# Attention heads on half the array: two heads, or two score maps, issued by turns on the two halves

## The chip, the cores and the metric

The kernel runs on one core of a Trainium2 chip. Times are device microseconds (us) of that core for one execution of the whole program; the time of a kernel is the median of its runs. The profile is a recording of one further execution. In it the engines are called PE (TensorE, matmuls), PEld (the weight loads of TensorE), DVE (VectorE), ACT (ScalarE), POOL (GpSimd) and SP (SyncE, which here issues the DMA transfers); "SPq" is SP's queue. L715 is line 715 of the kernel.

## The reference, cut to what matters

Two unrelated models run one after the other on 256 tokens of width 1024: `first_block` (called block 1 below) and `second_block` (block 2). Block 1 has two layers; in each, three kinds of attention work on one projection of the input, and their outputs, side by side, go through `w_o`. Only this part of block 1 is touched:

```python
def first_block(x, ...):
    h = x
    for i in range(DEPTH):                       # DEPTH = 2
        u = h @ w_in[i]
        u_mla, u_diff, u_sb = jnp.split(u, [MLA_IN, MLA_IN + DIFF_IN], axis=-1)
        y_mla = mla_mixer(u_mla, ...)            # 4 heads, 64 values a head
        y_diff = diff_mixer(u_diff, ...)         # 4 heads, two maps of 64 rows each, 128 values a head
        y_sb = sb_mixer(u_sb)                    # 4 heads of 64
        mix = jnp.concatenate([y_mla, y_diff, y_sb], axis=-1) @ w_o[i]
        h = layer_norm(DEEPNORM_ALPHA * h + mix, ln1_g[i], ln1_b[i])
        ffn = grouped_moe(h, ...)                # 16 experts
        ...

# diff_mixer, one head:
        a = attn_map(q1, k[0]) - lam * attn_map(q2, k[1])   # two softmax maps
        return jnp.einsum('bhqk,bhkd->bhqd', a, v)          # then an rms norm over 128 values

# sb_mixer (stick-breaking), one head:
        z = jnp.einsum('bhqd,bhkd->bhqk', qb, k) * scale
        log_fail = jnp.where(strict, jax.nn.log_sigmoid(-z), 0.0)
        later = lax.cumsum(log_fail, axis=3, reverse=True) - log_fail
        w = jnp.where(strict, jnp.exp(jax.nn.log_sigmoid(z) + later), 0.0)
        return jnp.einsum('bhqk,bhkd->bhqd', w, v)
```

The mask lets a query of the first 128 tokens see only the first 128 keys, so a score map is 128 queries x 256 keys for the later half and 128 x 128 for the earlier: 384 columns on 128 partitions.

## The kernel before

`mixers(l)` in block 1 makes the attention of layer l. Scores and values are fp32 matmuls (two records each in the trace, merged as x2); projections are products of operands split into a high and a low part, three matmuls each (`mm3`, lines 272 to 274).

**The heads as units.** Each head is a generator: `mla` and `sb` heads in turn first, then the four `diff` heads. A unit yields after each of its steps. A multi-latent head (`mla`) has three steps: scores and softmax; three transposes (`turn`, line 297) and a copy to SBUF (line 650); values. A stick-breaking head (`sb`) has scores with a mask product added (lines 715 to 718) and a log-sigmoid on ACT and DVE; the sums over later keys (lines 728 to 730) and an exponential; values (lines 736 and 737). A difference head (`diff`) has its first map's scores and softmax, its second map's, the combination on DVE, the transposes, the values and the sum of squares by ACT, and the product that sums over the partitions (line 704) with the norm. `scores` is on lines 631 and 632, `values` on 654 and 655, the bias add of a difference map on 686, `softmax` on 636 to 642.

**Halves of the array.** A stick-breaking head has 64 channels, so its scores contract over 64 rows, `qk[r]` with r the upper or the lower 64 partitions; the two maps of a difference head lie on the two halves in the same way. The values of a multi-latent or a stick-breaking head are 64 columns wide, and their output goes to the upper or lower 64 partitions `o[r]` of its own PSUM bank.

**What is drawn between the steps.** `flow(units, DM)` keeps DM = 3 units alive and takes a step of each in turn. After each step, `filling()` gives FM[l] steps on average (0.7 in layer 0, 0.6 in layer 1): first `diff_v` and `diff_in` (the projections that the difference heads need), then `project`, the product with w_o, one row block of the heads at a time in the order WO_ORDER as soon as `heads` has them. `diff(h)` draws on `filling()` until its own projection is there. In layer 0 the steps also draw 0.5 of a step of `t5`, which builds the position bias.

**Order, PSUM, weights.** The order of the code is what a scheduler starts from; it decides each engine's own order. `aux()` gives one of four PSUM banks to every score, transpose, sum or value tile; projections have the four others. Weights arrive by DMA in slots of SBUF, issued by SP in order, and are split into high and low by ACT (line 236) and DVE or POOL (line 267) some way ahead. `drop("mla")`, in the last stick-breaking head's last step, frees the four slots that the attention holds, and weight loads go there next. After `filling()` has run out come the layer norm, the expert stage and, after two layers, block 2.

## Time and profile before

| | |
|---|---|
| median of 3 runs | 1607.31 us (1604.68 to 1607.84) |
| the profiled execution | 1608.48 us, of which the span of the trace is 1606.7 us |
| PE busy | 1535.0 us, 96% of the span, 10998 matmul records |
| DVE busy | 824.1 us, 51% |
| ACT busy | 645.3 us, 40% |
| POOL busy | 201.0 us, 13% |
| DMA | 216 GB/s read and written over the span |

The attention heads of block 1 run from 54 to 152 us in the first layer and from 486 to 575 us in the second. A span is counted from the first to the last record of the trace; the execution's own time has 1.8 us more. Busy shares are means over stages that have different limits, and a matmul's end is modelled, so that the duration of a matmul record overlaps the next one's; the distance from one start to the next is what a matmul holds the engine for.

### The profile page before, as it was taken

Reading aid. Unit: us, or ns where it says so; the run is one execution under the profiler, and the core shown is the slowest. Engines: PE = TensorE matmul, PEld = TensorE weight load, DVE = VectorE, ACT = ScalarE, POOL = GpSimd, SP = SyncE. Lnnn points to the kernel's source line nnn. Section 1 sums busy time; section 2 is a strip of 40 time slices with the busy share of each in tenths; the row PEclk is TensorE's granted clock in tenths of the full one; section 3 lists DMA queues with packets and bytes.
Section 4 is the critical chain, followed back from the end, with each engine's and each line's share of the span. In section 5 each row is a group of like instructions: output and inputs, shape, how many; then the busy total and the mean of one; then the engine's idle time right before and its main releaser. Section 6 shows DMA issues by size and latency. Waiting matters only on the chain.

```text
span 1606.7 us, 26861 instructions
## 1 busy us (share of the span) xinstructions
PE 1535.0 (96%) x10998; PEld 1170.3 (73%) x10998; DVE 824.1 (51%) x1624; ACT 645.3 (40%) x1309; POOL 201.0 (13%) x236
## 2 busy tenths in 40 slices
PE   7999999989799999998997899899999999999999
PEld 7788744444287876454436787588999998799998
DVE  6677612212345772131216776536666666576665
ACT  5466411111136642110115674545444455554443
POOL 0130100000101001000003631301111023220000
PEclk9999999999999999999999999689999999999999
DMA  8335899999462489999943111025555452254540
GB/s 348 140 131 186 338 407 421 380 421 421 145 239 71 159 315 356 422 382 419 421 206 140 66 54 56 1 83 191 173 184 184 157 192 79 79 180 164 184 156 27
DMA packets 50034, 348.77 MB, mean 217 GB/s; under 512 B 5616, under 2 KB 6896, under 8 KB 8688
## 3 DMA queue, kind: packets, MB, share of 16 engines
q1 hardware_dynamic: 49904, 346.97, 56.2%
q8 instruction: 90, 1.47, 0.4%
q14 instruction: 40, 0.33, 0.1%
HBM read 345.90 MB, written 1.05 MB: 216 GB/s over the span
## 4 chain that ended last, share of the span: by engine, by line
PE 45%; DVE 4%; ACT 2%; POOL 1%; issue 1%; DVEq 0%; POOLq 0%; ACTq 0%
PE bank L274 10%; PE bank L272 10%; PE bank L273 10%; PE bank L1033 3%; PE bank L1067 2%; DVE ring L267 1%; PE aux L1507 1%; PE aux L297 1%; PE bank L994 1%; PE aux L1491 1%; PE aux L2008 1%; PE bank L1639 1%; ACT ring L236 1%; PE bank L1769 1%; PE aux L1986 1%
## 5 line engine op out<-in xcount | busy, mean ns | idle before, releaser
L236 ACT ACTIVATE ring<-ring 128x1024 fp32r<-128x1024 f32 (+3 forms) x188 | 185.8, 994 | 188.6 <-PE bank L274 166.6
L267 DVE TENSOR_TENSOR ring<-ring,ring 128x1024 fp32r<-128x1024 f32 x145 | 180.4, 1244 | 93.5 <-ACT ring L236 93.1
L272 PE MATMUL bank<-uh,ring 128*128 128x272 f32 (+1 forms) x744 | 218.6, 294 | 2.3 <-ACT ring L236 2.3
L274 PE MATMUL bank<-uh,ring 128*128 128x272 f32 (+1 forms) x744 | 215.5, 290 | 4.2 <-DVE ring L267 3.7
L273 PE MATMUL bank<-ul,ring 128*128 128x272 f32 (+1 forms) x744 | 215.0, 289 | 0.0
L274 PEld LDWEIGHTS bank<-uh,ring 128*128 128x128 f32 x744 | 141.4, 190 | 6.0 <-DVE ring L267 5.6
L272 PEld LDWEIGHTS bank<-uh,ring 128*128 128x128 f32 x744 | 141.3, 190 | 5.1 <-ACT ring L236 2.5
L273 PEld LDWEIGHTS bank<-ul,ring 128*128 128x128 f32 x744 | 141.2, 190 | 0.9 <-issue 0.2
L274 PE MATMUL bank<-rh,ring 128*128 128x272 f32 (+1 forms) x496 | 141.6, 286 | 0.0
L272 PE MATMUL bank<-rh,ring 128*128 128x272 f32 (+1 forms) x496 | 141.4, 285 | 0.0
L273 PE MATMUL bank<-rl,ring 128*128 128x272 f32 (+1 forms) x496 | 140.9, 284 | 0.0
L1039 DVE TENSOR_TENSOR hid<-hid,bank 128x512 f32<-128x512 f32 x16 | 11.0, 687 | 186.4 <-PE bank L1033 173.7
L273 PEld LDWEIGHTS bank<-rl,ring 128*128 128x128 f32 x496 | 93.8, 189 | 0.0
L272 PEld LDWEIGHTS bank<-rh,ring 128*128 128x128 f32 x496 | 93.2, 188 | 0.0
L274 PEld LDWEIGHTS bank<-rh,ring 128*128 128x128 f32 x496 | 93.0, 187 | 0.0
L267 POOL TENSOR_TENSOR ring<-ring,ring 128x1024 fp32r<-128x1024 f32 x6 | 14.5, 2436 | 574.4 <-ACT ring L236 574.4
L1257 POOL TENSOR_TENSOR fr<-fr 128x272 f32<-128x272 f32 (+1 forms) x64 | 40.2, 629 | 287.3 <-DVE fr L245 283.4
L245 DVE SCALAR_TENSOR_TENSOR big<-bank,gs,big 128x512 fp32r<-128x512 f32 x32 | 24.0, 750 | 99.2 <-ACT big L236 97.5
L267 DVE TENSOR_TENSOR ring<-wsp,ring 128x1024 fp32r<-128x1024 f32 x41 | 52.8, 1287 | 26.1 <-ACT ring L236 26.1
L236 ACT ACTIVATE ring<-wsp 128x1024 fp32r<-128x1024 f32 x41 | 43.4, 1058 | 55.4 <-PE bank L274 54.2
L236 ACT ACTIVATE big<-bank,gs 128x512 fp32r<-128x512 f32 x32 | 22.0, 688 | 108.0 <-PE bank L1067 107.7
L994 PE MATMUL bank<-P,hnat 128*128 128x128 f32 x512 | 63.6, 286 | 0.0
(677 smaller groups left out, 3431.4 us busy)
## 6 DMA issues: line engine op xcount, KB each, us to landing
ring<-w_ff SPq DMA_DIRECT2D x50, 1024.0 KB, 4.9
ring<-w_down SPq DMA_DIRECT2D x34, 1024.0 KB, 12.9
ring<-w_up SPq DMA_DIRECT2D x30, 1024.0 KB, 13.0
ring<-w_gate SPq DMA_DIRECT2D x29, 1024.0 KB, 10.4
big<-w_gate SPq DMA_DIRECT2D x24, 1024.0 KB, 16.4
big<-w_up SPq DMA_DIRECT2D x18, 1024.0 KB, 10.9
big<-w_down SPq DMA_DIRECT2D x17, 1024.0 KB, 11.8
wsp<-w_ff SPq DMA_DIRECT2D x14, 1024.0 KB, 4.8
```

The source lines that it names most:

```text
L236: return self.nc.scalar.activation(out, in_, func, **kw)
L245: return (eng or self.nc.vector).scalar_tensor_tensor(out, in0, s, in1, op0=op0, op1=op1, **kw)
L267: (eng or self.nc.vector).tensor_sub(l, src, h.bitcast(F32))
L272: mm(out, lhs[0], rhs[0], start=first, stop=False)
L273: mm(out, lhs[0], rhs[1], start=False, stop=False)
L274: mm(out, lhs[1], rhs[0], start=False, stop=last)
L297: self.nc.tensor.transpose(out, in_, self.ident[:k, :k])
L994: mm(b[:, j * M2:(j + 1) * M2], h[:, t, (k + j) * 128:(k + j + 1) * 128], P[:, t], start=t == 0, stop=t == 1)
L1033: mm(b[e * 64:e * 64 + CAP], xg[:, k, e * CAP:(e + 1) * CAP], w[:, (2 * k + e) * 512:(2 * k + e + 1) * 512], start=k == 0, stop=k == 7)
L1067: mm(yb[n][e * 64:e * 64 + CAP], hT[:, k, e * 64:e * 64 + CAP], w[:, o:o + 512], start=k == 0, stop=k == 3)
L1257: nc.gpsimd.tensor_mul(r, r, r)
L1491: nc.tensor.matmul(b[:, :N2], qw[r, j, self.hcols(t)], qw[r, 4], start=True, stop=True)
```

## The change

The heads of a kind go in pairs as one unit: `mla(hp)` and `sb(hp)` take heads 2hp and 2hp + 1, and a step of a difference head now issues the scores of both maps. `scores` and `values` take lists: first the 256-column matmuls of both halves, then the 128-column ones of both, so that neighbours in the code lie on different halves of the array. The values of a pair go to the two halves of one PSUM bank, and are split into high and low by one copy and one subtraction over 128 partitions, where two heads had one each over 64. The multi-latent units keep the scores of a pair in two steps, and the transposes in two; a stick-breaking pair keeps its two sum steps. The exponentials of the four multi-latent heads each have a place of their own (`me`, four in place of two). There are 38 unit steps in place of 48 in a layer, and FM goes from 0.7 and 0.6 to 0.88 and 0.75.

```diff
--- before.py
+++ after.py
@@ -58,7 +58,7 @@
 PJ = 3
 PL = 2
 PN = 2
-FM = (0.7, 0.6)
+FM = (0.88, 0.75)
 WPA = ((1, 3, 5, 7, 9, 11), ())
 WO_ORDER = [0, 1, 6, 7, 2, 3, 4, 5]
 T5_THR = [-90, -63, -45, -31, -22, -15, -11, -7, -6, -5, -4, -3, -2, -1, 0,
@@ -487,7 +487,7 @@
             vv = p1.tile([128, 2, 512], F32, name="vv")
             slot = self.slot(hold="mla")
             cn = slot[:, 0:768].rearrange("p (a s) -> p a s", a=3)
-            me = [slot[:, 768 + i * 384:768 + (i + 1) * 384] for i in range(2)]
+            me = [slot[:, i * 384:(i + 1) * 384] for i in range(4)]
             slot = self.slot(hold="mla").rearrange("p (a h s) -> p a h s", a=2, h=4)
             kt, qt = slot[:, 0], slot[:, 1]
             slot = self.slot(hold="mla")
@@ -627,10 +627,13 @@
                                     self.drop("hT")
                             yield
 
-            def scores(q, k, s):
-                mm(s[:, 0:256], q[:, 128:256], k, start=True, stop=True)
-                mm(s[:, 256:384], q[:, 0:128], k[:, 0:128], start=True, stop=True)
-                return s[:, 0:384]
+            def scores(qs, ks, ss):
+
+                for q, k, s in zip(qs, ks, ss):
+                    mm(s[:, 0:256], q[:, 128:256], k, start=True, stop=True)
+                for q, k, s in zip(qs, ks, ss):
+                    mm(s[:, 256:384], q[:, 0:128], k[:, 0:128], start=True, stop=True)
+                return [s[:, 0:384] for s in ss]
 
             def softmax(s, e):
 
@@ -650,26 +653,31 @@
                 nc.scalar.copy(PT, tp[:, :384])
                 return PT
 
-            def values(out, v, cols, PT):
-                mm(out[:, 0:256], v[:, 0, cols], PT[:, 0:256], start=True, stop=False)
-                mm(out[:, 128:256], v[:, 1, cols], PT[:, 256:384], start=False, stop=True)
-
-            def mla(h_):
-                s = scores(qt[:, h_], kt[:, h_], self.aux())
-                nc.vector.memset(self.masked(s), NEG)
-                e = me[h_ % 2]
-                rs = softmax(s, e)
-                self.ts(e[:, 0:256], e[:, 0:256], rs[:, 0:1])
-                self.ts(e[:, 256:384], e[:, 256:384], rs[:, 1:2])
-                yield
-                PT = turn(e)
-                yield
+            def values(outs, v, cols, PTs):
+                for out, cc, PT in zip(outs, cols, PTs):
+                    mm(out[:, 0:256], v[:, 0, cc], PT[:, 0:256], start=True, stop=False)
+                for out, cc, PT in zip(outs, cols, PTs):
+                    mm(out[:, 128:256], v[:, 1, cc], PT[:, 256:384], start=False, stop=True)
+
+            halves = [slice(64 * j, 64 * j + 64) for j in range(2)]
+
+            def mla(hp):
+                PTs = []
+                for h_ in (2 * hp, 2 * hp + 1):
+                    s, = scores([qt[:, h_]], [kt[:, h_]], [self.aux()])
+                    nc.vector.memset(self.masked(s), NEG)
+                    e = me[h_]
+                    rs = softmax(s, e)
+                    self.ts(e[:, 0:256], e[:, 0:256], rs[:, 0:1])
+                    self.ts(e[:, 256:384], e[:, 256:384], rs[:, 1:2])
+                    yield
+                for h_ in (2 * hp, 2 * hp + 1):
+                    PTs.append(turn(me[h_]))
+                    yield
                 o = self.aux()
-                r = slice(64 * (h_ % 2), 64 * (h_ % 2) + 64)
-                values(o[r], vm, slice(64 * h_, 64 * h_ + 64), PT)
-                self.split(yh[r, h_ // 2], yl[r, h_ // 2], o[r, 0:256])
-                if h_ % 2:
-                    heads.append(h_ // 2)
+                values([o[r] for r in halves], vm, [slice(64 * h_, 64 * h_ + 64) for h_ in (2 * hp, 2 * hp + 1)], PTs)
+                self.split(yh[:, hp], yl[:, hp], o[:, 0:256])
+                heads.append(hp)
                 yield
 
             def diff(h_):
@@ -679,13 +687,11 @@
                     next(t5)
                 q, k = dqk[h_][:, 0], dqk[h_][:, 1]
                 es = []
-                for i in range(2):
-                    r = slice(64 * i, 64 * i + 64)
-                    s = scores(q[r], k[r], self.aux())
+                for s in scores([q[r] for r in halves], [k[r] for r in halves], [self.aux(), self.aux()]):
                     e = p2.tile([128, 384], F32, name="de", bufs=4)
                     nc.vector.tensor_add(e, s, self.bias[:, h_])
                     es.append((e, softmax(e, e)))
-                    yield
+                yield
                 (e1, r1), (e2, r2) = es
                 lr = p2.tile([128, 2], F32, name="lr", bufs=3)
                 self.ts(lr, r2, lam)
@@ -696,7 +702,7 @@
                 PT = turn(e1)
                 yield
                 o = self.aux()
-                values(o, vv, slice(128 * h_, 128 * h_ + 128), PT)
+                values([o], vv, [slice(128 * h_, 128 * h_ + 128)], [PT])
                 sq = p2.tile([128, S], F32, name="osq", bufs=2)
                 self.act(sq, o[:, 0:256], AF.Square)
                 yield
@@ -708,37 +714,33 @@
                 heads.append(2 + h_)
                 yield
 
-            def sb(h_):
-                hp, j = h_ // 2, h_ % 2
-                r = slice(64 * j, 64 * j + 64)
-                z = self.aux()[:, 0:384]
-                mm(z[:, 0:256], qk[r, 1, hp, 0:128], qk[r, 0, hp], start=True, stop=False)
-                mm(z[:, 0:128], self.ident, self.c["future"], start=False, stop=True)
-                mm(z[:, 256:384], qk[r, 1, hp, 128:256], qk[r, 0, hp, 128:256], start=True, stop=False)
-                mm(z[:, 256:384], self.ident, self.c["future"], start=False, stop=True)
-                g = sbg[h_ % 2]
-                self.act(g, z, AF.Abs)
-                self.act(g, g, AF.Exp, scale=-1.0)
-                self.act(g, g, AF.Ln, bias=1.0)
-                self.stt(g, z, 0.0, g, OP.min, OP.subtract)
-                f = sbf[h_ % 2]
-                nc.vector.tensor_sub(f, g, z)
-                yield
-                lt_ = self.aux()
-                mm(lt_[:, 0:256], self.utri, f[:, 0:256], start=True, stop=False)
-                mm(lt_[:, 128:256], self.ones, f[:, 256:384], start=False, stop=True)
-                mm(lt_[:, 256:384], self.utri, f[:, 256:384], start=True, stop=True)
-                nc.vector.tensor_add(g, g, lt_[:, 0:384])
-                self.act(g, g, AF.Exp)
-                yield
+            def sb(hp):
+                zs = [self.aux()[:, 0:384] for _ in range(2)]
+                for o, q, kc in ((slice(0, 256), slice(0, 256), slice(0, 128)), (slice(256, 384), slice(128, 256), slice(128, 256))):
+                    for z, r in zip(zs, halves):
+                        mm(z[:, o], qk[r, 1, hp, kc], qk[r, 0, hp, q], start=True, stop=False)
+                    for z in zs:
+                        mm(z[:, o.start:o.start + 128], self.ident, self.c["future"], start=False, stop=True)
+                for z, g, f in zip(zs, sbg, sbf):
+                    self.act(g, z, AF.Abs)
+                    self.act(g, g, AF.Exp, scale=-1.0)
+                    self.act(g, g, AF.Ln, bias=1.0)
+                    self.stt(g, z, 0.0, g, OP.min, OP.subtract)
+                    nc.vector.tensor_sub(f, g, z)
+                yield
+                for g, f in zip(sbg, sbf):
+                    lt_ = self.aux()
+                    mm(lt_[:, 0:256], self.utri, f[:, 0:256], start=True, stop=False)
+                    mm(lt_[:, 128:256], self.ones, f[:, 256:384], start=False, stop=True)
+                    mm(lt_[:, 256:384], self.utri, f[:, 256:384], start=True, stop=True)
+                    nc.vector.tensor_add(g, g, lt_[:, 0:384])
+                    self.act(g, g, AF.Exp)
+                    yield
                 o = self.aux()
-                cols = slice(64 * h_, 64 * h_ + 64)
-                mm(o[r, 0:256], vs[:, 0, cols], g[:, 0:256], start=True, stop=False)
-                mm(o[r, 128:256], vs[:, 1, cols], g[:, 256:384], start=False, stop=True)
-                self.split(yh[r, 6 + hp], yl[r, 6 + hp], o[r, 0:256])
-                if j:
-                    heads.append(6 + hp)
-                if h_ == 3:
+                values([o[r] for r in halves], vs, [slice(64 * h_, 64 * h_ + 64) for h_ in (2 * hp, 2 * hp + 1)], sbg)
+                self.split(yh[:, 6 + hp], yl[:, 6 + hp], o[:, 0:256])
+                heads.append(6 + hp)
+                if hp:
                     self.drop("mla")
                 yield
 
@@ -797,7 +799,7 @@
                 yield from project()
 
             fill = filling()
-            units = [u(h_) for h_ in range(4) for u in (mla, sb)] + [diff(h_) for h_ in range(4)]
+            units = [u(hp) for hp in range(2) for u in (mla, sb)] + [diff(h_) for h_ in range(4)]
             due = due5 = 0
             for _ in flow(units, DM):
                 due, due5 = due + FM[l], due5 + T5B
```

What the engines are given stands in their orders. The names: `dqk` is q and k of a difference head, `ring_3380` (before) and `ring_3368` (after) the slot with the stick-breaking q, k and v, `ring_3379` and `ring_3367` that of the multi-latent ones, `prm` the constants, `PT` transposed weights of the attention, `de` the exponentials of a difference head, `vv` its values, `osq` its squares, and `bank<-` rows are projections.

PE in the second layer, the first scores of the attention. Before, those of one multi-latent and one stick-breaking head:

```order
L631 MATMUL aux<-ring_3379 128x256
L632 MATMUL aux<-ring_3379 128x128
L715 MATMUL aux<-ring_3380 128x256
L716 MATMUL aux<-prm 128x128
L717 MATMUL aux<-ring_3380 128x128
L718 MATMUL aux<-prm 128x128
L272 MATMUL bank<-ring_3739,big_3335 128x512
```

and after:

```order
L633 MATMUL aux<-ring_3367 128x256
L635 MATMUL aux<-ring_3367 128x128
L721 MATMUL aux<-ring_3368 128x256 x2
L723 MATMUL aux<-prm 128x128 x2
L721 MATMUL aux<-ring_3368 128x128 x2
L723 MATMUL aux<-prm 128x128 x2
L272 MATMUL bank<-ring_3737,big_3323 128x512
```

The multi-latent head is as before (96 channels, which fill more than half of the rows); of the stick-breaking scores two heads' matmuls stand next to each other, then two mask products.

PE in the first layer, from the transposes ahead of the last difference head's scores. Before:

```order
L297 MATMUL aux<-prm,de 128x128 x3
L631 MATMUL aux<-dqk 128x256
L632 MATMUL aux<-dqk 128x128
L654 MATMUL aux<-PT,vv 128x256
L655 MATMUL aux<-PT,vv 128x128
L654 MATMUL aux<-PT,vv 128x256
L655 MATMUL aux<-PT,vv 128x128
L631 MATMUL aux<-dqk 128x256
L632 MATMUL aux<-dqk 128x128
L272 MATMUL bank<-wsp_1358,ring_162 128x512
L273 MATMUL bank<-wsp_1358,ring_162 128x512
L274 MATMUL bank<-wsp_1358,ring_163 128x512
```

and after:

```order
L297 MATMUL aux<-prm,de 128x128 x3
L633 MATMUL aux<-dqk 128x256 x2
L635 MATMUL aux<-dqk 128x128 x2
L658 MATMUL aux<-PT,vv 128x256
L660 MATMUL aux<-PT,vv 128x128
L273 MATMUL bank<-wsp_1383,ring_162 128x512
L274 MATMUL bank<-wsp_1383,ring_163 128x512
L272 MATMUL bank<-wsp_1383,ring_162 128x512
L710 MATMUL aux<-osq,prm 128x256
L273 MATMUL bank<-wsp_1383,ring_162 128x512
```

Before, the last head's two maps stand apart, with values between them; after, they are one group behind the transposes, and the first sum of squares follows. From these scores to the last head's own transposes there are 15 projections and two sums of squares before, and 17 projections, one values group and one sum of squares after.

PE in the second layer, values of the first two multi-latent heads. Before, with the first stick-breaking head's between them:

```order
L654 MATMUL aux<-PT,ring_3380 64x256
L655 MATMUL aux<-PT,ring_3380 64x128
L274 MATMUL bank<-ring_3742,big_3336 128x512
L736 MATMUL aux<-big_3381,ring_3380 64x256
L737 MATMUL aux<-big_3381,ring_3380 64x128
L654 MATMUL aux<-PT,ring_3380 64x256
L655 MATMUL aux<-PT,ring_3380 64x128
```

and after, two value pairs that stand next to each other:

```order
L658 MATMUL aux<-PT,ring_3368 64x256 x2
L660 MATMUL aux<-PT,ring_3368 64x128 x2
L658 MATMUL aux<-PT,ring_3368 64x256
L272 MATMUL bank<-big_3323,ring_3855 128x256
L658 MATMUL aux<-PT,ring_3368 64x256
L660 MATMUL aux<-PT,ring_3368 64x128 x2
```

The first pair stands whole; in the second, a projection stands between the two 256-column matmuls.

## Rows read from the trace of the kernel before

**Rows 1.** Windows of the two attention stretches: busy us of each engine, with record counts.

```profile
core 0: us, PE busy (x) PEld busy (x) DVE busy (x) ACT busy (x) POOL busy (x), PEclk, DMA share, GB/s
54.00:152.00 98.00, 97.68 (x582) 81.37 (x581) 70.75 (x190) 60.64 (x151) 20.62 (x10) 1.00 0.38 138
486.00:575.00 89.00, 88.47 (x506) 72.55 (x505) 56.82 (x124) 57.38 (x131) 6.41 (x4) 1.00 0.38 133
```

**Rows 2.** PE's waits from 54 to 152 us: us in total, times, longest.

```profile
PE aux L297 <- DVE de L245: 0.3, 1, 0.3
```

**Rows 3.** PE's waits from 486 to 575 us.

```profile
PE bank L272 <- ACT ring L236: 0.5, 1, 0.5
```

**Rows 4.** Timeline of PE, full-array matmuls in fp32 and projections: start, us, instruction.

```profile
104.78 0.59 PE L728 MATMUL aux<-ring,prm 128*128 128x256 f32 x2
105.21 0.38 PE L729 MATMUL aux<-ring,prm 128*128 128x128 f32 x2
105.43 0.39 PE L730 MATMUL aux<-ring,prm 128*128 128x128 f32 x2
...
105.77 0.28 PE L273 MATMUL bank<-ring,wsp 128*128 128x256 f32 x1
105.89 0.28 PE L274 MATMUL bank<-ring,wsp 128*128 128x256 f32 x1
```

**Rows 5.** Timeline of PE, the scores of one stick-breaking head.

```profile
56.67 0.70 PE L715 MATMUL aux<-ring 64*128 64x256 f32 x2
57.30 0.49 PE L716 MATMUL aux<-prm 128*128 128x128 f32 x2
57.72 0.48 PE L717 MATMUL aux<-ring 64*128 64x128 f32 x2
```

**Rows 6.** Timeline of PE, the two maps of a difference head.

```profile
117.42 0.70 PE L631 MATMUL aux<-dqk 64*128 64x256 f32 x2
...
118.27 0.38 PE L272 MATMUL bank<-ring,wsp 128*128 128x256 f32 x1
118.58 0.70 PE L631 MATMUL aux<-dqk 64*128 64x256 f32 x2
```

**Rows 7.** Timeline of PE, the values of one multi-latent head.

```profile
72.93 0.65 PE L654 MATMUL aux<-PT,ring 128*64 128x256 f32 x2
73.41 0.38 PE L655 MATMUL aux<-PT,ring 128*64 128x128 f32 x2
73.72 0.50 PE L272 MATMUL bank<-wsp,ring 128*128 128x512 f32 x1
```

**Rows 8.** Timeline of PE in the experts, matmuls alternating between column halves.

```profile
217.08 3.65 PE L1067 MATMUL bank<-ring,hidT 128*64 128x512 f32 x16
220.56 1.89 PE L1067 MATMUL bank<-big,hidT 128*64 128x512 f32 x8
```

**Rows 9.** Timeline of PE in block 2, tiles of 32 rows by 32 columns.

```profile
1004.49 0.69 PE L1678 MATMUL bank<-ring,ring 32*32 32x32 f32 x32
```

**Rows 10.** Waits of SP's queue from 95 to 135 us.

```profile
SPq L231 <- PE aux L737: 4.3, 1, 4.3
```

**Rows 11.** DMA issues from 40 to 200 us: KB each, median us to landing.

```profile
big<-w_o SPq DMA_DIRECT2D x1, 1024.0 KB, 8.6
```

**Rows 12.** Timeline from the last scores of the last difference head, first layer.

```profile
137.66 0.38 PE L632 MATMUL aux<-dqk 64*128 64x128 f32 x2
...
138.08 0.56 DVE L686 TENSOR_TENSOR de<-aux,big 128x384 f32<-128x384 f32 x1 [0.73 <-PE aux L632]
...
138.68 0.61 DVE L639 TENSOR_REDUCE st<-de 128x1 f32<-128x256 f32 x2
...
139.13 0.51 ACT L236 ACTIVATE de<-de,st 128x256 f32<-128x256 f32 x1 [0.64 <-DVE st L639]
...
141.47 0.74 DVE L245 SCALAR_TENSOR_TENSOR de<-de,st 128x256 f32<-128x256 f32 x2
...
142.39 0.49 PE L297 MATMUL aux<-prm,de 128*128 128x128 f32 x3
```

**Rows 13.** PE's waits in the first layer's experts, from 200 to 432 us.

```profile
PE bank L297 <- PEq L1081: 4.1, 1, 4.1
```

## The prediction, made before the changed kernel was run

> **What bounds the kernel now.** I read first the windows of the two stretches in which the attention heads of block 1 run, one for each of its two layers. TensorE (PE) is busy for 97.68 of 98.00 us in the first and 88.47 of 89.00 in the second, at the full granted clock; VectorE (DVE) is busy for 72 and 64% of the time, ScalarE for 62 and 64% [rows 1]. A busy PE need not be a PE at its peak, so I then read what PE waited for: 0.3 us in the whole of the first stretch [rows 2] and 0.5 in the second [rows 3]. So PE sets the pace of both, and time taken off PE there is time off the kernel, unless a wait comes out that PE's own work had covered.
>
> Then I read single matmuls on the timeline, by the distance from one start to the next. On the full array an fp32 matmul over 256 columns takes 0.43 us (104.78 to 105.21), one over 128 columns 0.22 (105.21 to 105.43), and a projection matmul over 256 columns 0.12 (105.77 to 105.89) [rows 4]. The scores of one stick-breaking head look different: the 64-row matmul over 256 columns takes 0.63 us, the mask matmul over 128 columns behind it 0.42 [rows 5]. So each time PE goes from a 64-row to a 128-row matmul or back, some 0.20 us are added. The two score maps of a difference head pay that too: from the start of map 1 (117.42) to the projection behind it (118.27) are 0.85 us for 0.43 + 0.22 = 0.65 of streaming, and that projection holds PE for 0.31 in place of 0.12 before map 2 begins [rows 6]. Matmuls into 64 columns pay a little less: 0.79 us in all for 0.65 [rows 7], and the rest on either side. I take 0.19 us for a change of either kind.
>
> The experts show what pairing does with column halves: 16 records of 512 columns, which alternate between the halves, take 3.48 us (217.08 to 220.56), so 0.217 each [rows 8]. An fp32 matmul leaves two records, so a record over 256 columns takes 0.215 alone [rows 4] and one over 512 would take 0.43: two run at a time. For row halves that share all columns the trace has no such place. The nearest are block 2's 32x32 tiles, of which two differ in rows and in columns: 32 records in 0.69 us are 22 ns each, the tail of the last one included [rows 9], where 32 columns at 0.215 per 256 would take 27. These overlap too.
>
> **The change part by part.** No matmul and no weight is added. Three things change on PE.
>
> First, fewer changes of array form. Counting in PE's order from the first mask-step matmul of a layer's attention to its layer norm, PE goes between full array, row halves and column halves 45 times before and 26 times after in the first layer, 42 and 24 times in the second. 37 changes at 0.19 us are 7.0 us.
>
> Second, column halves side by side. In the first layer all four value pairs have equal matmuls next to each other: each hides one head's 0.43 and 0.22, so 4 x 0.65 = 2.6 us. In the second layer three pairs do, and of the fourth only the 128-column halves (a projection stands between the others): 3 x 0.65 + 0.22 = 2.2 us. Together 4.8 us.
>
> Third, row halves side by side. First layer: the second stick-breaking pair 0.65, the first none (its second half waits for a bank and comes after the mask of the first), difference head 0 only 0.22, heads 1 to 3 0.65 each: 2.8 us. Second layer: two pairs and four heads, 6 x 0.65 = 3.9 us. Together 6.7 us, with bounds from nothing (no overlap) to 6.7 (as the column halves do). The 32x32 tiles are the nearest row and they overlap, so I take 6.7. The sum on PE is 7.0 + 4.8 + 6.7 = 18.5 us.
>
> The Trainium skill's page TensorE: Matmul & The Clock Gate, section Measured speedup vs the span model, gives 3.07 times for four row tiles; no run here shows that. By an estimate from it (3.07/4 of the ideal, so a pair in 0.65 of the serial time) row pairs would give 4.7 us in place of 6.7, and the sum would be 16.5 us.
>
> The new numbers FM change nothing by themselves: 48 unit steps at 0.7 and 0.6 call for 33.6 and 28.8 steps of projections, 38 steps at 0.88 and 0.75 for 33.4 and 28.5. The merged y split issues 4 instead of 8 copies on ScalarE and 4 instead of 8 subtractions on DVE in a layer; that lies beside PE and counts as nothing. The weight loads behind the dropped attention slots are ordered after the last stick-breaking values, where SP, the queue that issues the loads, waited 4.3 us [rows 10]. In PE's new order these values come behind 35 more projections than before, but PE has by then saved about as much, so the loads (the second half of w_o, and two of the next stage) are issued at about the same time; ScalarE splits the first of them behind head 0's sum of squares, 48 projections and some 3 us of fp32 matmuls later, about 9 us, and w_o landed 8.6 us after its issue [rows 11]. A microsecond or two late would hold ScalarE, not PE, which has other products to do; I count nothing.
>
> What comes back is waits, because each pair puts two vector chains behind one step. Look at the last difference head of the first layer: the last score matmul of its second map starts at 137.66, the vector work goes from 138.08 to 142.21 (141.47 and 0.74), and PE takes up the transposes at 142.39, just as they are ready [rows 12]. In the new order 17 projections, the values of the head before and one sum of squares stand in that gap, against 15 projections and two sums of squares: with 0.65 and 0.43 us for the fp32 ones, some 0.6 us more cover. But both maps now queue behind one step: one more bias add (0.6, from 138.08 to 138.68), two more reductions (0.6), and the first map's exponentials ahead on ScalarE (0.5 and less for the second). That is 1.2 to 2 us more chain, so 0.6 to 1.4 of wait; I take 1 us in each layer. Difference head 0 of the first layer, where PE waits already [rows 2], now has head 1's scores directly behind its own, four maps in the queue in place of one: 2 us. Head 2 there and the bank of the first stick-breaking pair: 0.5 us each. Together 5 us; bounds are nothing (the projections cover all) and the 24 us of the last rival.
>
> Net: 18.5 - 5 = 13.5 us. The profiled execution took 1608.48 us (span 1606.7 and 1.8 around it); 1608.5 - 13.5 is 1595. The median of the runs, 1607.31, is 1.2 below it, so I say **1594 us**.
>
> **Rivals.** *All covered*: no new wait, the whole 18.5: 1607.3 - 18.5 = 1589. For it speaks that almost nothing waits now; against it that the last head's transposes have no time to spare [rows 12].
>
> *Row halves run one after the other*: two row tiles share all output columns, and no row shows two of those at once. Then 6.7 of the 18.5 go; PE is slower and fewer chains come out, say 3 us: 18.5 - 6.7 - 3 = 9, so 1598 to 1599.
>
> *Given back in the experts*: 100 MB of weights stream in there, and if that stream sets their end and its start does not move, both layers' gains vanish: 1607, no change. Against it: PE's longest wait in 232 us of experts, 4.1 us, is for its own sequencer at the overflow branch, ahead of any wait for a weight [rows 13]; the loads are let go by PE and DVE, which come earlier.
>
> *The vector engines set the pace*: at each of the twelve paired units with scores (eight difference heads, four stick-breaking pairs) the second head's chain comes out in full. From the rows of one map (add 0.6, two reductions 0.6, exponentials 0.5 and somewhat less [rows 12]) that is about 2 us a unit, 24 us in all, and 1607.3 - 18.5 + 24 makes 1613 us: slower. It decides once a unit exposes more than (18.5 + 3.2) / 12 = 1.8 us. Against it: the new order leaves 17 or more projections between a pair's scores and its next step on PE at all twelve, and DVE is idle for over a quarter of both stretches [rows 1]. The Trainium skill's page TensorEngine Tiling (Array Packing), section PSUM Bottleneck, warns of this in general: tiling speeds up TensorE, not the emptying of PSUM. No run here shows it so far.
>
> **How the numbers follow.** Chances: the forecast 0.46, all covered 0.14, row halves in turn 0.20, given back 0.13, vector pace 0.07. The forecast's own range is 1590 to 1598. From 1588 (all covered, with a microsecond for the scatter of the runs, 1604.68 to 1607.84) to 1602 (row halves in turn, with 3 us more waits) the first three cases lie, which is 0.80. What a measurement can tell from no change is about 0.2%, 3.2 us, so faster means below 1604.1: the first three cases and a little of the fourth, 0.82; the same: 0.11; slower: 0.07.
>
> **What would show it.** Right: paired records of the score and value matmuls start within some 10 ns of each other; 256-column pairs take 0.43 us as one; the distance from a pair's first start to the next projection is near 0.85 for both maps together; the layer norms of block 1 begin some 5 us (first layer) and 13 us (second, both gains) earlier, and the rest of the span is shifted by as much. Wrong: paired row records start 0.21 us apart (row halves in turn); PE's waits in the two stretches sum to 10 us or more, for DVE at the transposes (vector pace); or the gain is there at the layer norms and gone at the end of the experts.

## The result, and the profile of the changed kernel

The changed kernel takes 1587.85 us (median of 4 runs, 1583.12 to 1589.72) against 1605.99 us before (4 runs, 1601.35 to 1607.84): ratio 0.989, 95% interval 0.9866 to 0.9914, so 14 to 22 us less. Its profiled execution has a span of 1587.9 us.

I cut both traces at the same places. A layer's stretch runs from the last projection ahead of the first scores to the router's first matmul behind the layer norm; the experts run from their first gather matmul to their last combining one. In microseconds, with the runs that follow further down:

| kernel | layer 0 | experts 0 | layer 1 | median, ratio to before |
|---|---|---|---|---|
| before, two traces | 126.4, 126.4 | 238.1, 237.7 | 116.2, 116.3 | |
| changed, two traces | 121.3, 122.2 | 234.8, 234.8 | 107.4, 107.5 | 1587.85, 0.9890; again 1590.43, 0.9910 |
| all by head | 122.6 | 236.5 | 110.4 | 1593.31, 0.9928 |
| difference heads only | 124.6 | 235.4 | 113.6 | 1601.07, 0.9978 |
| other heads only | 123.7 | 238.1 | 111.0 | 1598.79, 0.9959 |
| own bank | 117.7 | 234.8 | 107.5 | 1585.27, 0.9876 |
| masks last | 121.6 | 234.7 | 106.7 | 1586.82, 0.9881 |
| both of these | 117.0 | 236.7 | 106.7 | 1583.26, 0.9866 |
| bias added twice | 129.2 | 237.9 | 112.6 | 1601.42, 0.9980 |
| by head but for the masks | 122.4 | 234.9 | 109.3 | 1589.29, 0.9912 |
| old FM | 122.3 | 237.7 | 112.0 | 1594.82, 0.9951 |

The two traces of a kernel agree within 0.1 us in layer 1 and within 0.9 in layer 0: the stretches tell effects apart that the medians, with intervals some 4 to 8 us wide, do not.

First a difference head of the changed kernel in layer 1, on PE's timeline, to be held against [rows 6]:

```profile
507.47 0.70 PE L633 MATMUL aux<-dqk 64*128 64x256 f32 x4
508.01 0.39 PE L635 MATMUL aux<-dqk 64*128 64x128 f32 x4
508.33 0.39 PE L273 MATMUL bank<-big,ring 128*128 128x256 f32 x1
```

Both maps together take 0.86 us from their first start to the projection; one map took 0.85. The values of two heads, against one head's in [rows 7]:

```profile
79.71 0.65 PE L658 MATMUL aux<-ring,ring 128*64 128x256 f32 x4
80.19 0.39 PE L660 MATMUL aux<-ring,ring 128*64 128x128 f32 x4
80.51 0.38 PE L272 MATMUL bank<-ring,wsp 128*128 128x256 f32 x1
```

0.80 us for two heads, 0.79 for one: the second matmul of a pair is hidden whole, in rows as in columns.

The trace of the kernel before already had one such place, which the prediction does not use. In its second layer the values of stick-breaking head 0 and multi-latent head 1, which lie on different column halves, stand next to each other, each head's 256 columns ahead of its 128 and one head behind the other; in its first layer the values of two heads on the same half do:

```profile
497.88 0.43 PE L736 MATMUL aux<-big,ring 128*64 128x256 f32 x1
497.90 0.43 PE L654 MATMUL aux<-PT,ring 128*64 128x256 f32 x1
...
498.37 0.27 PE L737 MATMUL aux<-big,ring 128*64 128x128 f32 x1
...
498.69 0.50 PE L272 MATMUL bank<-ring,big 128*128 128x512 f32 x1
```

```profile
69.10 0.65 PE L654 MATMUL aux<-PT,ring 128*64 128x256 f32 x2
...
69.80 0.59 PE L736 MATMUL aux<-ring,ring 128*64 128x256 f32 x2
...
70.54 0.50 PE L272 MATMUL bank<-wsp,ring 128*128 128x512 f32 x1
```

On different halves both heads take 0.81 us, on the same half 1.44.

PE's waits from 50 to 150 us and from 460 to 575 us, which answer to [rows 2, 3]:

```profile
PE bank L274 <- DVE wsp L267: 0.9, 1, 0.9
PE aux L721 <- DVE big L395: 0.8, 1, 0.8
PE bank L273 <- DVE wsp L267: 0.2, 1, 0.2
```

```profile
PE bank L297 <- DVE hnat L245: 0.5, 1, 0.5
PE aux L633 <- ACT dqk L624: 0.5, 1, 0.5
```

None is at a transpose of a difference head. The place of [rows 12] in the new order, the last head of layer 0:

```profile
133.00 0.39 PE L635 MATMUL aux<-dqk 64*128 64x128 f32 x4
...
133.42 1.02 DVE L692 TENSOR_TENSOR de<-aux,big 128x384 f32<-128x384 f32 x2 [0.40 <-PE aux L635]
...
137.64 0.74 DVE L245 SCALAR_TENSOR_TENSOR de<-de,st 128x256 f32<-128x256 f32 x2
...
138.52 0.52 PE L297 MATMUL aux<-prm,de 128*128 128x128 f32 x3
```

The vector chain of both maps runs from 133.42 to 138.38, 5.0 us against 4.1 for the second map before; from the last scores to the transposes PE has 5.5 us of work, against 4.7. The transposes are again just on time.

The wait for `big` is another matter. The first stick-breaking pair, and the windows around it (columns as in [rows 1]):

```profile
55.12 0.48 PE L721 MATMUL aux<-ring 64*128 64x128 f32 x2
56.43 0.67 PE L721 MATMUL aux<-ring 64*128 64x256 f32 x2 [0.83 <-DVE big L395]
```

```profile
53.00:56.00 3.00, 2.60 (x14) 1.78 (x13) 2.98 (x6) 0.61 (x4) 1.84 (x1) 1.00 0.87 328
56.00:59.00 3.00, 2.57 (x11) 1.93 (x11) 2.03 (x9) 0.87 (x4) 0.00 (x0) 0.77 0.95 373
59.00:62.00 3.00, 3.00 (x15) 2.52 (x13) 0.72 (x3) 2.31 (x7) 0.00 (x0) 0.66 0.17 61
```

The pair's second half needs a second PSUM bank, which a step of the position bias holds until DVE has read it. PE stands still for 0.83 us, and behind that the granted clock reads 0.77 and 0.66 where it was 1.00: part of these windows ran at 1.2 GHz, the lower of the two levels.

### The profile page after: what moved, and what is told of

The parts are those of the page before. It is cut to its first block, busy times and chain, and to the rows that moved or that the text cites. A ratio compares the mean times of both kernels' runs of the same rounds, so it can differ in the third digit from the quotient of the medians.

```text
span 1587.9 us, 26849 instructions
## 1 busy us (share of the span) xinstructions
PE 1515.7 (95%) x10998; PEld 1159.3 (73%) x10998; DVE 820.2 (52%) x1616; ACT 639.0 (40%) x1301; POOL 202.5 (13%) x236
## 4 chain that ended last, share of the span: by engine, by line
PE 46%; DVE 5%; ACT 2%; POOL 1%; issue 1%; DVEq 0%; POOLq 0%; ACTq 0%
PE bank L274 10%; PE bank L272 10%; PE bank L273 10%; PE bank L1035 3%; PE bank L1069 2%; DVE ring L267 1%; PE aux L1509 1%; PE aux L297 1%; PE aux L1493 1%; PE bank L996 1%; PE aux L2010 1%; ACT ring L236 1%; PE bank L1771 1%; PE bank L1641 1%; PE aux L1988 1%
## 5 line engine op out<-in xcount | busy, mean ns | idle before, releaser
L236 ACT ACTIVATE ring<-ring 128x1024 fp32r<-128x1024 f32 (+4 forms) x183 | 180.1, 992 | 187.2 <-PE bank L274 167.9
L274 PE MATMUL bank<-rh,ring 128*128 128x272 f32 (+1 forms) x480 | 137.1, 286 | 0.0
L272 PE MATMUL bank<-rh,ring 128*128 128x272 f32 (+1 forms) x480 | 136.9, 285 | 0.0
L273 PE MATMUL bank<-rl,ring 128*128 128x272 f32 (+1 forms) x480 | 136.4, 284 | 0.0
L272 PEld LDWEIGHTS bank<-rh,ring 128*128 128x128 f32 x480 | 90.2, 188 | 0.0
L274 PEld LDWEIGHTS bank<-rh,ring 128*128 128x128 f32 x480 | 90.0, 187 | 0.0
L1069 PE MATMUL bank<-ring,hidT 128*64 128x512 f32 x280 | 63.1, 596 | 0.7 <-ACT hidT L1054 0.7
```

The lines of the kernel that those rows point to most:

```text
L236: return self.nc.scalar.activation(out, in_, func, **kw)
L272: mm(out, lhs[0], rhs[0], start=first, stop=False)
L273: mm(out, lhs[0], rhs[1], start=False, stop=False)
L274: mm(out, lhs[1], rhs[0], start=False, stop=last)
L1069: mm(yb[n][e * 64:e * 64 + CAP], hT[:, k, e * 64:e * 64 + CAP], w[:, o:o + 512], start=k == 0, stop=k == 3)
```

## The experiments

**The changed kernel again**, no edit.

> The changed kernel once more, timed in five rounds, for the size of the gain and for a second trace. If the gain is what the first trace shows in the two attention stretches (5.1 us from the start of the scores to the end of layer 0's projections and 8.8 us in layer 1, 13.9 together), the ratio to before is near 0.991 (14 us), and the further 4.9 us of the first pair of traces (2.6 ahead of the attention, 3.2 and 1.1 in the experts, -2.0 behind them) do not all come again. If the whole 18 us belong to the change, the ratio is near 0.989 again and the same pieces come again.

1590.43 us against 1605.29 (ratio 0.991, 0.9894 to 0.9926). The stretches came again: 122.2 and 107.5, together 12.9 to 14.0 us less than before. Of the rest, the experts of layer 0 came again (234.8 against 238.1 and 237.7), the start did not: it ends at 52.0 and 51.3 in the two traces of the changed kernel, at 53.9 and 51.2 in those of before. The 2.6 us of the first pair were scatter.

**All by head.**

```diff
-                for q, k, s in zip(qs, ks, ss):
-                    mm(s[:, 0:256], q[:, 128:256], k, start=True, stop=True)
                 for q, k, s in zip(qs, ks, ss):
+                    mm(s[:, 0:256], q[:, 128:256], k, start=True, stop=True)
                     mm(s[:, 256:384], q[:, 0:128], k[:, 0:128], start=True, stop=True)
...
-                for o, q, kc in (...):
-                    for z, r in zip(zs, halves):
+                for z, r in zip(zs, halves):
+                    for o, q, kc in (...):
                         mm(z[:, o], qk[r, 1, hp, kc], qk[r, 0, hp, q], start=True, stop=False)
-                    for z in zs:
                         mm(z[:, o.start:o.start + 128], self.ident, self.c["future"], start=False, stop=True)
```

(`values` is edited like `scores`.)

> Pairs as in the changed kernel (same units, steps, FM, banks), but the matmuls of a pair are issued by head: both of one half, then both of the other; stick-breaking scores head by head with each mask product behind its matmul. If the gain is the overlap of halves and the fewer changes of array form: a difference head keeps 0.22 of 0.65 us of overlap (7 x 0.43 lost = 3.0), the value pairs likewise (7 x 0.43 = 3.0), the stick-breaking pairs lose all (3 x 0.65 = 2.0) and gain 14 changes of form at 0.19 (2.7): 10.7 us slower than the changed kernel, about 1598.5, and matmuls of one head start 0.2 us or more apart. If the gain comes from fewer steps and another mix with the projections, it stays within 2 us of the changed kernel, about 1588.

Neither: 1593.31, 2.9 us slower than the changed kernel (1590.43) where 10.7 and nothing were expected. Layer 1 loses 3.0 us. The stick-breaking pairs, with a full-array product between any two half matmuls, lost their overlap; by the expectation's own prices these two pairs (0.65 each) and six more changes of form in this layer (0.19 each) make 2.4 of the 3.0. The difference heads and the values kept their overlap, which the run by head but for the masks shows alone.

**Difference heads only, and the other heads only**: the kernel before with only `diff` changed, and the changed kernel with `diff` put back.

```diff
-                for i in range(2):
-                    r = slice(64 * i, 64 * i + 64)
-                    s = scores(q[r], k[r], self.aux())
+                halves = [slice(64 * j, 64 * j + 64) for j in range(2)]
+                ss = [self.aux(), self.aux()]
+                for r, s in zip(halves, ss):
+                    mm(s[:, 0:256], q[r][:, 128:256], k[r], start=True, stop=True)
+                for r, s in zip(halves, ss):
+                    mm(s[:, 256:384], q[r][:, 0:128], k[r][:, 0:128], start=True, stop=True)
...
-FM = (0.7, 0.6)
+FM = (0.76, 0.65)
```

> The kernel before with the difference heads alone changed: both maps' scores in one step, by turns (FM 0.76 and 0.65 for 44 steps). By the sum: overlap 0.22 + 3 x 0.65 + 4 x 0.65 = 4.8 us and some 14 changes of form at 0.19 = 2.7, together 7.5 us: about 1598.5. If the waits that I charged to the difference heads (4 us) appear here, 3.5 us remain: about 1602.5, and PE waits for DVE at the transposes of the last head of each layer.

> The changed kernel with the difference heads put back (a step for each map, FM 0.8 and 0.69 for 42 steps), so that only the multi-latent and stick-breaking pairs are left. By the sum: column halves 4.8, row halves 0.65 + 1.3 = 2.0, some 23 changes of form at 0.19 = 4.4, together 11.1 us: about 1595. With the difference heads' 7.5 this would make the 18.5 of the sum; if the two parts add up to clearly less than the whole change gives, something else of the change pays too.

Each gives less than its sum: 4.2 us (ratio 0.9967 to 0.9989) and 6.5 us (0.9946 to 0.9972) by the medians. In the stretches they give 1.8 and 2.6, and 2.7 and 5.2: 12.3 us together, where the whole gives 13 to 14. So the parts about add up. The difference heads alone removed 11 changes of form in place of 14, and in layer 0 PE waited 2.6 us at three places ahead of the layer norm, none of them a difference head's; in layer 1 this kernel lost the overlap of values at 497.88 us that the kernel before had, since its two heads no longer stand together. The other heads alone had the wait for the second bank (0.8 us) and 2.5 us of further waits in layer 0, where the kernel before has 1.3 in all.

**Own bank, masks last, and both.**

```diff
-                zs = [self.aux()[:, 0:384] for _ in range(2)]
+                zs = [(self.bank() if l == 0 and hp == 0 and j else self.aux())[:, 0:384] for j in range(2)]
```

```diff
-                for o, q, kc in (...):
+                cuts = (...)
+                for i, (o, q, kc) in enumerate(cuts):
                     for z, r in zip(zs, halves):
-                        mm(z[:, o], qk[r, 1, hp, kc], qk[r, 0, hp, q], start=True, stop=False)
+                        mm(z[:, o], qk[r, 1, hp, kc], qk[r, 0, hp, q], start=i == 0, stop=False)
+                for i, (o, q, kc) in enumerate(cuts):
                     for z in zs:
-                        mm(z[:, o.start:o.start + 128], self.ident, self.c["future"], start=False, stop=True)
+                        mm(z[:, o.start:o.start + 128], self.ident, self.c["future"], start=False, stop=i == 1)
```

> The changed kernel with one bank moved: in layer 0 the second half of the first stick-breaking pair takes a PSUM bank of the projections, two of which are unused then, instead of waiting for one of the four of the attention, which a bias step holds. If the wait (0.8 us at the second half's first matmul) and the fall of the granted clock behind it (0.77 and 0.66 in the six microseconds from 56 to 62, which cost about 1.6 us) are the reason that layer 0 gives 4 to 5 us and layer 1 8.8: layer 0's stretch from the first scores to the router falls from 121.3 to 122.2 to about 118.5, the clock stays at 1.00 there, and the kernel is 3 us faster than the changed one. If the wait moves on to the next bank, or the clock falls anyway, the stretch stays above 120.5.

> The changed kernel with the stick-breaking pairs' four row-half matmuls ahead of their four mask products: two changes of array form fewer in each of the four pairs, and the 128-column halves directly behind the 256-column ones; the same matmuls. If a change of form costs 0.19 us: 8 x 0.19 = 1.5 us less on PE, seen as about 0.75 us in layer 1's stretch (107.4 to 106.7) and the same in layer 0. If what looks like a price of the change is the start of any matmul with other weights, nothing changes (107.4 stays).

> Both of the edits: the bank and the mask products last. If both reasons hold, they add up: 3 + 1.5 us, layer 0's stretch near 117.7, layer 1's near 106.7, and some 4.5 us less than the changed kernel, near 1585. If the first wait only moves, about 1588.

All three came by the stretches as expected from the reasons, but for layer 0 with the masks last: 121.6 us lies between the changed kernel's 121.3 and 122.2, so the 0.75 us expected there do not show beside the bank's wait. The medians alone do not tell the first two from the changed kernel. With its own bank layer 0 takes 117.7 us, 3.6 to 4.5 less, and layer 1 stays at 107.5. Since the two halves now write to banks of different names, the timeline shows them apart, and the windows keep their clock:

```profile
54.38 0.48 PE L721 MATMUL aux<-ring 64*128 64x256 f32 x1
54.39 0.48 PE L721 MATMUL bank<-ring 64*128 64x256 f32 x1
```

```profile
56.00:59.00 3.00, 3.00 (x23) 2.66 (x20) 2.68 (x13) 2.24 (x9) 0.00 (x0) 1.00 1.01 377
59.00:62.00 3.00, 3.00 (x16) 2.59 (x16) 2.79 (x9) 2.83 (x7) 0.00 (x0) 1.00 0.29 109
```

The row halves start 10 ns apart. With the masks last, layer 1 takes 106.7 in place of 107.4 to 107.5 for four changes of form fewer: 0.19 us each. Both edits together take 1583.26 us (ratio 0.9846 to 0.9887), the lowest median of all, and there the masks do show in layer 0: 117.0 in place of 117.7.

**Bias added twice**: `nc.vector.tensor_add(e, s, self.bias[:, h_])` stands twice in `diff`.

> The changed kernel with the bias add of each score map of the difference heads done twice by DVE (the second writes the same values): 16 more adds of 0.5 us in two layers, two in each head's chain, 1.1 us each head. If the vector engines set the pace in the pairs, all eight heads come out: 8 to 9 us slower. If only the last head of each layer has no slack (its transposes start 0.1 us after their data is ready), 1 us in each layer: 2 us slower, and PE waits about 1 us for DVE at these transposes and nowhere else. If projections cover every chain with room, nothing.

1601.42, some 11 us slower than the changed kernel by the ratios to before (0.9980 against 0.9910), and by none of the three ways. PE's waits in layer 1 (484 to 600 us):

```profile
PE bank L297 <- DVE hnat L245: 3.6, 2, 2.3
PE bank L273 <- DVE ring L267: 0.2, 1, 0.2
```

None is at a pair; in layer 0 one of 1.1 us is at the last head's transposes, as the second theory had it. The 3.6 us stand in each layer at the layer norm: the scheduler, given longer chains, put 11 of layer 1's 24 matmuls of the next stage (`aux<-ring,ring`) ahead of the last ones with w_o, so 13 are left for PE to do while the norm is made, where the changed kernel has 24. Behind the norm's waits the granted clock fell as well, to 0.50 from 160 to 165 us and to 0.74 from 580 to 586. The order moved with the cost, so the run does not price the chains by themselves; it shows that the pairs did not begin to wait.

**By head but for the masks**: `scores` and `values` by head as above, the stick-breaking scores by turns.

> The changed kernel with the difference heads' scores and all values issued by head (256 columns and then 128 of one half, then the same of the other), the stick-breaking scores by turns as they are. If each half of the array takes its own matmuls in order and independently of the other, as the 13 ns between the two heads' starts in the kernel issued by head suggest, nothing is lost: layer 1's stretch stays at 107.5 and the kernel within 1 us of the changed one. If turns are needed, as my sum of the overlap by neighbours assumed, 0.43 us are lost at each of 14 pairs, 6 us in all, 3 of them in layer 1 (110.5).

1589.29 (ratio 0.9895 to 0.9928), not told from the changed kernel. A difference head of layer 1, each map's 256 and 128 columns issued before the other map's:

```profile
509.99 0.71 PE L633 MATMUL aux<-dqk 64*128 64x256 f32 x4
510.53 0.39 PE L634 MATMUL aux<-dqk 64*128 64x128 f32 x4
510.85 0.39 PE L273 MATMUL bank<-big,ring 128*128 128x256 f32 x1
```

Again 0.86 us, and both 256-column matmuls start before either of 128 columns: PE took the third matmul ahead of the second. Layer 1 is 1.8 us longer, of which 1.4 are waits: 2.6 us in its new order against 1.2 (new are 1.2 at two sums of squares and 0.4 at another product; 0.5 at the norm is gone). One value pair of this layer lost its overlap, since ACT's copy of its second head's `PT` ended only at 500.5 us; the other value pairs and the difference heads kept what they have in the changed kernel.

**Old FM**: `FM = (0.7, 0.6)` in the changed kernel.

> The changed kernel with the old FM (0.7 and 0.6 steps of projections for each of the 38 unit steps, so 20% fewer beside the heads and more behind them). If the numbers only keep the mix as it was, and the mix covers the pairs' vector chains, fewer projections between the steps bring out waits at the transposes and values: some 3 to 6 us slower than the changed kernel, with PE waiting for DVE and ACT in the two stretches. If the chains have cover to spare, within 1 us.

1594.82 (ratio 0.9951, 0.9937 to 0.9966, where the changed kernel has 0.991). Layer 0 is as long as in the changed kernel, layer 1 4.5 us longer. PE's waits there:

```profile
PE aux L297 <- DVE wsp L241: 1.3, 1, 1.3
PE bank L272 <- ACT ring L236: 1.0, 2, 0.7
PE aux L633 <- ACT dqk L624: 0.7, 1, 0.7
PE bank L297 <- DVE hnat L245: 0.5, 1, 0.5
```

3.5 us of waits at these places in place of 1.0, one of them (1.3) for a pair's softmax. Two changes of form more explain 0.4; the other 1.6 us I did not trace.

**The kernel before again**, no edit.

> The kernel before once more, for its second trace. If the stretches are as steady as those of the changed kernel, layer 0 from the first scores to the router takes 126.4 and layer 1 116.2 again within 1 us, while the start, the experts and block 2 move by up to 3 us each with the granted clock.

1603.84 us, stretches 126.4 and 116.3. PE's wait at the overflow branch in the experts of layer 0, to be held against [rows 13], here first and then in the changed kernel:

```profile
PE bank L297 <- PEq L1081: 3.7, 1, 3.7
```

```profile
PE bank L297 <- PEq L1083: 2.7, 1, 2.7
```

## Why the prediction was right, and where its steps were not

It said 1594, with a range of 1588 to 1602; 1587.85 lies a little outside the range and the repeat, 1590.43, in it. The mechanism and the sign are right, and in the two stretches the net is right: 13.5 us forecast, 12.9 to 14.0 measured. That the net came so close is luck in part: the losses that came are others than those forecast, of near their size, and the sum is 0.65 us too high.

**The sum on PE, 18.5 us, holds but for 0.65.** With the bank's wait taken away the stretches give 8.7 + 8.7 = 17.4 us. I counted as new the overlap of a value pair in layer 1 that the kernel before already had (497.88 us), so 0.65 go; with its own bank the first pair of layer 0 overlaps too and saves two changes of form, so for that kernel 1.0 come back: 18.9. PE's waits in the two whole stretches, layer norms included, grow from 2.5 us before to 3.7; 18.9 less these 1.2 is 17.7, near the 17.4. The price of a change of form, 0.19, is what the masks last showed. That row halves overlap as column halves do was the open point; it is shown by the 10 ns. The estimate of 4.7 us in place of 6.7, worked out from the Trainium skill's page TensorE: Matmul & The Clock Gate, section Measured speedup vs the span model, is too low here: the second map is hidden whole.

**The waits, 5 us, were put in the wrong place.** The step that failed is the term for new waits: 1 us at the last difference head of each layer and 2 us at head 0 of layer 0 never came. I had the chain grow by 1.2 to 2 us and the cover by 0.6; the chain grew by 0.8, since DVE and ACT work on the two maps at once, and the cover by 0.8. The first stick-breaking pair's bank, for which I charged a wait of 0.5 us, costs 3.6 to 4.5. In the first trace the terms make 3.6: the wait 0.8, the pair's lost overlap 0.65, two changes of form that stay 0.4, and, by an estimate from the windows from 56 to 62, 1.7 for the clock (0.77 and 0.66 of 3 us each). The overlap and the changes of form were in the sum, which gives this pair nothing; the clock was in no term. So what came in place of the 5 us is 1.9 of waits (4.4 in the two whole stretches against 2.5) and the clock's 1.7, together 3.6.

**Counting overlap by neighbours alone was too strict.** I counted 0.22 of 0.65 where the 256-column matmuls of a pair do not stand next to each other, and the expectations of the runs by head rest on the same count. These runs show that turns are not needed as long as nothing on the full array stands between, and the kernel before had shown it at 497.88 us, where two heads, one behind the other in the program, take 0.81 us. The Trainium skill's page TensorE: Matmul & The Clock Gate, section The mechanism, has matmuls start strictly in program order; these traces differ: L654 starts at 497.90, ahead of L737 at 498.37, which stands before it in the program.

**The rest of the gain lies outside the change.** The experts of layer 0 end 3 us shorter in both traces. The wait at the overflow branch is 2.7 us (2.8 in the second trace) where it was 4.1 and 3.7. Behind the longer wait the granted clock was 0.76 from 328 to 330 us and 0.59 from 330 to 333 in the kernel before; behind the shorter it stayed at 1.00. Why the branch waits less is open: it was not tried. It does not go with the pairs: the other heads only has a wait of 4.2 us and 238.1 for these experts, both edits together 3.0 and 236.7. The rivals: row halves in turn is refuted; given back in the experts is refuted too, since the weight stream took nothing back; vector pace did not come at any pair; all covered (1589) is the nearest in time, but not in its reason, since about 4 us did come back.

## What to carry to other kernels

Matmuls that fill half the array are worth putting next to each other twice over: the second is hidden, and two changes of form at 0.19 us go. Put nothing full-array between them; the order within the group matters little. Before pairing, look for what a pair needs at once that one did not, above all a second PSUM bank: here the missing bank took back 3.6 to 4.5 of the 8.7 us that the layer gains with it, through a wait, an overlap that did not come, and in these traces a stretch at the lower clock. And keep the share of filler per step when steps become fewer: leaving it cost 4.5 us in one layer, and nothing that shows in the other.

## What was not expected of the hardware

PE started a matmul of one half ahead of others that stand before it in the program and lie on the other half: in the run by head but for the masks three records stand in the program between the first records of the two maps' 256-column matmuls, and yet all four of their records form one group from 509.99 us and the 128-column ones the next, from 510.53. And a wait of 0.83 us was followed by a granted clock of 0.77 and 0.66 in the windows from 56 to 62 us; in the second trace of the changed kernel, where the profile puts the wait at 0.3 us, and in the kernel with the masks last, where it is 0.9, the clock reads 0.50 in both windows. With the second bank, and so without the wait, it reads 1.00 (own bank, and both edits).

But the wait alone does not decide it. The old FM has the same wait, and its clock stayed up:

```profile
PE aux L721 <- DVE big L395: 0.8, 1, 0.8
```

```profile
56.00:59.00 3.00, 2.31 (x12) 1.73 (x13) 2.27 (x10) 1.33 (x5) 0.00 (x0) 1.00 1.00 371
59.00:62.00 3.00, 3.00 (x20) 2.69 (x19) 2.00 (x7) 2.94 (x10) 0.00 (x0) 1.00 0.26 96
```

So did that of the other heads only (0.8 us, and 1.00 in all windows from 50 to 65 us), while all by head, whose profile shows no such wait, reads 0.60 and 0.50. What else it takes is open.
